# Work moved from VectorE to ScalarE and GpSimd, gate tiles last, retention states in two groups, in a hybrid decoder layer on one core

## Chip, cores and metric

One core of one Trainium2 chip runs the whole program in one launch. The metric is device microseconds of one execution. The kernel before takes 1557.36 us (median of 3 runs, 1556.4 to 1557.76).

## What is computed

One layer over 304 tokens: 16 meta tokens and 256 prompt tokens, and 8 samples of 4 new tokens. Columns of one input projection are split between two groups of heads (RWKV-7, 16 heads of 64; retention, 4 heads of 256), whose outputs go through one output projection; then a SwiGLU network. All in float32. The inner part, cut:

```python
z = rms_norm(x, norm_mix) @ w_in                      # 2048 -> 3360 + 4096 columns
o_a, S_a = rwkv7_mixer(z[..., :RWKV_COLS], z_prev, S_a0, ...)
o_b, S_b = retention_mixer(z[..., RWKV_COLS:], S_b0, pos, prompt)
h = x + concatenate([o_a, o_b]) @ w_out
h = h + (silu(hn @ w_gate) * (hn @ w_up)) @ w_down    # hn = rms_norm(h, norm_ffn), 2048 -> 5632 -> 2048
# RWKV-7, per step:  S = S * w_t + (S @ a_t) b_t + v_t k_t ;  out = S @ r_t
# retention, per chunk:
o = (q @ k.T * dmask) @ v + (q @ S) * inter_scale
S_new = exp(log_gamma * C) * S + (k * k_scale).T @ v
o = o * rsqrt(mean(o * o) + eps) * silu(g)
```

The outputs are y for prompt and samples, the last projected rows and the new states of both groups.

## The kernel before, in words

Activations lie transposed (features on partitions, the 304 tokens along the free dimension). The weights of all projections stand in one long array `big` in the order of their use, and are streamed by SP's queue in loads of 1024 columns (512 KB, tiles `wr`, three buffers, `load` at line 608). Each float32 weight is split: ScalarE casts 512 columns to a high half `wh` (`cast`, line 617), VectorE subtracts it from the weight and leaves a low half `wl` (`rest`, line 629). TensorE then makes three matmuls for each block of 128x128 weights: high x high, high x low activations, low x high (`main`, line 634). A piece of 512 columns is four blocks, 12 matmuls. In `main` the cast runs four pieces ahead; the subtraction follows in the middle of a piece and is needed two and a half pieces later.

`sequence` (line 103) gives the order of the output tiles. First come 59 tiles of the input projection: 3 for the LoRA inputs, then by `ORDER` (line 54) 3 tiles for each of 8 RWKV pairs of heads (p0 to p7), 6 for each retention head (r0 to r3: q, k, v), 2 for each head's gate (g0 to g3). After them come the output projection in two halves (the second needs the retention heads) and the feed-forward network.

Beside this main stream run the heads, as generators that give way at every `yield`. A planner (`Plan`, line 307) drafts the program first: it books each instruction with a duration on its engine's clock (`book`, line 348, for instance 265 + 2 n ns for a GpSimd product of n columns), steps a generator when its data are due, and lets the main stream go on otherwise. The order that comes out is written as it is; each engine works through its own queue in order. So a row of one engine that comes late holds whatever is queued behind it on that engine.

The parts that the change touches:
- `rsqrt` (line 705): a reciprocal root by an integer guess and two corrections, all on VectorE. Twelve calls are 288 wide (8 in `pair_out`, line 1297, and 4 in `ret`), 8 are 312 wide and have a floor in place of the affine first step (`pair`, line 906), one is 304 wide at the start, the others are 3 wide.
- `lora_weights` (line 870): splits a pair's LoRA weights in halves, twice for each pair, and loads the pair's sample states `s0`.
- `pair`: builds the padded operand `arp` (a and r, [128, 5, 2, 2, 64]) and multiplies it by `bku` to scores.
- `inverse` (line 1095): for each pair the inverse of triangular 64x64 blocks. VectorE reduces, then spreads a row by 15 shuffles in three groups of five; GpSimd makes two products or sums for each of them (30 rows of 5 to 75 columns); VectorE then masks, transposes and spreads the result (a 128x512 product), and TensorE multiplies.
- `sample` (line 1219): the sample tokens of a pair; VectorE scales `s0` there.
- `ret` (line 1379): a retention head. It loads four tiles of sample states (`s0r`, 512 KB each, by `states`, line 1390), multiplies q with them (16 matmuls into one PSUM tile), and later updates and stores the four tiles (`out_rts`). Head 0 starts after pair 3, head 1 after pair 5, heads 2 and 3 after pair 6, head h also after head h-2.

Since a wrapper (`Timed`, line 291) issues every instruction, all have one line in the profile, L302. Tiles of the heads lie in one arena, so their names there are `arena_dt.float` (or `arena_dt.float32r`); `acc` and `mm` are PSUM tiles of the main stream and of the heads.

Of the kernel before, what the change touches and what calls it, by code (L numbers as in the profile page):

```python
# [15 lines left out]
P = 128  # L16
# [3 lines left out]
META = 16  # L20
# [22 lines left out]
WARM = 10  # L43
BRIDGE = 4
# [9 lines left out]
ORDER = "p0 p1 g0 p2 r0 p3 p4 g1 p5 r1 p6 g2 p7 g3 r2 r3"  # L54
# [252 lines left out]
class Plan:  # L307
# [40 lines left out]
    def book(self, eng, what, a, k):  # L348
# [20 lines left out]
        else:  # L369
            part = out.shape[0] < P  # L370
            each = sum(math.prod(x.shape[1:]) == 1 for x in ins) if n > 1 else 0
            if eng == "DVE":
                big = max(math.prod(x.shape[1:]) for x in aps)
                per = 0.56 if what == "tensor_scalar" and ins[0].name not in self.banks else 1.05
                dur, tail = {"stream_shuffle": (148, 90), "transpose": (95 + 1.02 * n, 80), "tensor_reduce": (40 + 1.8 * big, 85),
                             "tensor_tensor_scan": (65 + 2.1 * n, 85)}.get(what, (62 + per * n + 67 * each, 83))
            elif eng == "ACT":
                dur, tail = 108 + 0.83 * n + 90 * each - 40 * (ins[0].name in self.banks), 94
            else:
                dur, tail = (60 + 0.85 * n, 60) if what == "memset" else (185 + 0.8 * n, 60) if what == "tensor_copy" else (265 + 2 * n, 60)  # L380
# [158 lines left out]
class Step:  # L539
# [165 lines left out]
    def rsqrt(self, src, scale, eps, floor=None, out=None):  # L705


        dve = self.dve
# [24 lines left out]
    def start(self):  # L733
# [3 lines left out]
        self.dve.memset(self.ones, 1.0)  # L737
        xh, xl = self.xh, self.xl
# [131 lines left out]
    def lora_weights(self, p, half, z):  # L870
# [4 lines left out]
        if not half:  # L875
            z["s0"] = self.t([P, NB, 64], "s0")
            self.sp.dma_start(z["s0"], self.I["s0w"][p])
# [5 lines left out]
        dve.tensor_sub(lo, lw, hi)  # L883
# [22 lines left out]
    def pair(self, p, z):  # L906
# [4 lines left out]
        while not all(("lora", i) in self.done for i in range(3)) or len(z) < 5:  # L911
            yield
# [6 lines left out]
        k, r, v, s0, (wh, wl) = z["k"], z["r"], z["v"], z["s0"], z["lora", 0]  # L919
# [46 lines left out]
        arp = self.t([P, NU, 2, 2, 64], "arp")  # L966
# [6 lines left out]
        pool.memset(arp[:, 0], 0.0)  # L973
        for hi, h in enumerate(HALF):
            pool.memset(arp[h, 1:, :, 1 - hi], 0.0)
# [15 lines left out]
        for hi, h in enumerate(HALF):  # L991
            act.copy(arp[h, 0, 0, hi, :META], ra[h, 0, :META])
            act.copy(arp[h, 1:, :, hi], units(ra[h]))
# [17 lines left out]
        for g in (1, 2), (3, 4), (0,):  # L1011
            pt = self.ps()
            n = 2 if g[0] else 1
            for j, u in enumerate(g):
                pe.matmul(pt[:, j * 2 * P:(j * 2 + n) * P], bku[:, u],
                          arp[:, u, :n].rearrange("p q h c -> p (q h c)"), start=True, stop=True)
# [21 lines left out]
        for i, h in enumerate(HALF):  # L1038
            act.copy(sc[h, :, 0, i, :], arp[h, :, 0, i, :])
# [7 lines left out]
        yield from self.units(p, sc, bkt, sv, sav, tt, arp, dl, o)  # L1047
# [47 lines left out]
    def inverse(self, mt):  # L1095
# [7 lines left out]
        pool.tensor_copy(x, cst("i16", 16)[:, None, :].to_broadcast([P, NU, 16]))  # L1103
        yield
# [4 lines left out]
        ems = []  # L1109
# [9 lines left out]
        for li in range(2):  # L1119
            em = self.t([P, NU, 64], "em")  # L1120
            pool.memset(em[:, NU - 1], 0.0)
            dve.tensor_mul(em[:, :NU - 1], mt[:, 1:],
                           cst("lvl", 128)[:, li * 64:(li + 1) * 64][:, None, :].to_broadcast([P, NU - 1, 64]))
            ems.append(em)
        yield
# [46 lines left out]
    def units(self, p, sc, bkt, sv, sav, tt, arp, dl, o):  # L1172
# [36 lines left out]
        for u in range(1, NU):  # L1209
            out = pt[:, (u - 1) * P:u * P]  # L1210
            pe.matmul(out, flat(sv, u), arp[:, u, 1].rearrange("p h c -> p (h c)"), start=True, stop=False)
# [7 lines left out]
    def sample(self, p, v, ax, axd, bs, d4, s0):  # L1219
# [10 lines left out]
        for hi, h in enumerate(HALF):  # L1230
            for b in range(2):
                act.copy(xs[h, b::2], pb[HALF[b], :, b, hi, :])

# [46 lines left out]
        dve.tensor_mul(s0, s0, d4.to_broadcast([P, NB, 64]))  # L1280
# [98 lines left out]
    def ret(self, h, q, k, v):  # L1379
# [50 lines left out]
        states()  # L1430
# [16 lines left out]
        pt = self.ps()  # L1447
        for g in range(2):
            for d in range(2):
                for j in range(4):  # L1450
                    b = 4 * g + j
                    pe.matmul(pt[32 * j:32 * j + 32, :RD], qz[:, d, b, :], s0s[b // 2][:, d, b % 2, :],
                              start=g + d == 0, stop=g + d == 2, tile_position=(0, 32 * j))

# [6 lines left out]
        qo = self.t([P, RD], "qo")  # L1461
        act.copy(qo, pt[:, :RD])
# [5 lines left out]
        act.copy(svh[0:32], svh[32:64].bitcast(F32))  # L1468

# [10 lines left out]


        for b2 in range(NB // 2):
            s0 = s0s[b2]
            vx = self.t([P, 2, RD], "vxr", F32R)
            for j in range(2):
                c = cst("bm128", 8)[:, 2 * b2 + j:2 * b2 + j + 1]
                if j:
# [282 lines left out]
```

## Time and profile before

| what | value |
|---|---|
| runs, median (3) | 1557.36 us |
| the profiled execution | 1558.99 us |
| its span, first to last instruction | 1557.1 us |
| TensorE's mean granted clock | 0.996 |
| weight loads | 409 of 512 KB and 8 of 256 KB |

The input projection with the heads takes about the first 587 us, the output projection follows, and from about 704 us on the feed-forward network. In a line of the waits stand: the engine and what it was to write, whom it waited for, then the sum in us, the number of waits and the longest. In a line of groups: line, engine, operation, out<-in, shape, count, busy us, mean ns of one, and idle time of the engine before them with what ended it. In a line of the timeline: start, length, engine, operation, count, and in brackets the idle time before it. In a line of stretches: the stretch and its length, then the busy time and count of PE, its weight loads (PEld), DVE (VectorE), ACT (ScalarE) and POOL (GpSimd), then the granted clock, the DMA share and GB/s.

### The profile page before, as it was taken

What the parts mean: (1) busy time and instruction counts of PE and PEld (TensorE: products, weight loads), DVE (VectorE), ACT (ScalarE), POOL (GpSimd) and SP (SyncE); (2) the same over time, 40 slices, a digit from 0 to 9 for tenths busy, and PEclk for the clock granted to TensorE, in tenths of its full rate; (3) what the DMA queues carried; (4) which work ended last, traced back from release to release, by engine and by line L of the source; (5) the groups of instructions that cost most, each with busy time, mean ns of one, the idle gap of its engine ahead of it and who ended that gap; (6) DMA issues with size and microseconds to landing.
All of it is one profiled execution on the core that took longest, in us unless ns stands there. A gap on an engine that the chain in (4) does not pass through costs nothing.

```text
span 1557.1 us, 30803 instructions
## 1 busy us (share of the span) xinstructions
PE 1535.6 (99%) x11388; PEld 1505.7 (97%) x11388; DVE 1102.0 (71%) x2590; ACT 821.4 (53%) x1795; POOL 179.2 (12%) x567
## 2 busy tenths in 40 slices
PE   9999999999999999999999999999999999999997
PEld 8999999998999999999999999999999999999997
DVE  7999888996999786676555565555565656565657
ACT  6766776766676555455444444444444444444445
POOL 0454415513143000000000000000000000000000
PEclk9999999999999999999999999999999999999999
DMA  7443443434545546755555555555555555555553
GB/s 249 154 136 119 127 130 120 115 107 152 181 143 176 170 143 238 243 167 161 164 173 163 174 156 172 162 165 169 168 163 172 164 166 164 171 166 166 161 176 118
DMA packets 76997, 252.48 MB, mean 162 GB/s; under 512 B 9392, under 2 KB 14640, under 8 KB 76848
## 3 DMA queue, kind: packets, MB, share of 16 engines
q1 hardware_dynamic: 76848, 250.52, 51.5%
q8 instruction: 90, 1.47, 0.4%
q14 instruction: 59, 0.48, 0.1%
HBM read 236.21 MB, written 14.28 MB: 161 GB/s over the span
## 4 chain that ended last, share of the span: by engine, by line
PE 85%; DVE 11%; issue 1%; ACT 1%; DMA 1%; POOL 0%; SPq 0%; DVEq 0%; ACTq 0%; POOLq 0%
PE acc L302 76%; PE mm L302 9%; DVE arena_dt.float L302 8%; DVE wl L302 3%; ACT arena_dt.float L302 1%; DMA arena_dt.float<-xT 0%; POOL arena_dt.float L302 0%; DMA arena_dt.float<-lora 0%; ACT wh L302 0%; DVE arena_dt.float32r L302 0%; DMA wr<-big 0%; ACT arena_dt.float32r L302 0%; SPq L302 0%; DVEq L1766 0%; ACT xh L302 0%
## 5 line engine op out<-in xcount | busy, mean ns | idle before, releaser
L302 PE MATMUL acc<-xh,wh 128*128 128x288 f32 (+2 forms) x2592 | 790.9, 305 | 0.0
L302 PE MATMUL acc<-xh,wl 128*128 128x288 f32 (+2 forms) x2592 | 769.9, 297 | 0.9 <-DVE wl L302 0.8
L302 PE MATMUL acc<-xl,wh 128*128 128x288 f32 (+2 forms) x2592 | 766.7, 296 | 0.0
L302 ACT CAST wh<-wr 128x512 fp32r<-128x512 f32 x826 | 501.6, 618 | 373.2 <-PE acc L302 343.3
L302 DVE TENSOR_TENSOR wl<-wr,wh 128x512 fp32r<-128x512 f32 x826 | 563.3, 690 | 114.5 <-ACT wh L302 112.1
L302 PEld LDWEIGHTS acc<-xh,wh 128*128 128x128 f32 x2592 | 487.7, 188 | 4.8 <-issue 1.5
L302 PEld LDWEIGHTS acc<-xl,wh 128*128 128x128 f32 x2592 | 486.9, 188 | 4.0 <-issue 0.7
L302 PEld LDWEIGHTS acc<-xh,wl 128*128 128x128 f32 x2592 | 486.0, 188 | 2.0 <-DVE wl L302 1.5
L302 PE MATMUL acc<-arena_dt.float32r,wh 128*128 128x288 f32 x1408 | 280.0, 294 | 0.4 <-ACT arena_dt.float32r L302 0.3
L302 PEld LDWEIGHTS acc<-arena_dt.float32r,wh 128*128 128x128 f32 x1408 | 225.5, 188 | 0.9 <-ACT arena_dt.float32r L302 0.6
L302 PE MATMUL acc<-arena_dt.float32r,wl 128*128 128x288 f32 x704 | 207.0, 294 | 0.0
L302 DVE TENSOR_TENSOR arena_dt.float<-acc,arena_dt.float 128x288 f32<-128x288 f32 (+4 forms) x181 | 72.7, 420 | 167.6 <-PE acc L302 167.3
L302 PE MATMUL mm<-arena_dt.float 128*128 128x128 f32 (+7 forms) x1072 | 168.4, 317 | 6.2 <-DVE arena_dt.float L302 4.9
L302 DVE TENSOR_TENSOR arena_dt.float<-arena_dt.float 128x288 f32<-128x288 f32 (+11 forms) x483 | 159.5, 354 | 11.7 <-ACT arena_dt.float L302 6.2
L302 DVE TENSOR_TENSOR arena_dt.float<-arena_dt.float,acc 128x288 f32<-128x288 f32 x208 | 94.4, 454 | 100.8 <-PE acc L302 100.6
L302 PEld LDWEIGHTS mm<-arena_dt.float 128*128 128x128 f32 (+1 forms) x1072 | 138.2, 182 | 20.6 <-issue 9.3
L302 ACT ACTIVATE arena_dt.float<-arena_dt.float 128x288 f32<-128x288 f32 (+6 forms) x200 | 85.0, 432 | 119.5 <-DVE arena_dt.float L302 118.2
L302 PEld LDWEIGHTS acc<-arena_dt.float32r,wl 128*128 128x128 f32 x704 | 132.7, 189 | 0.0
L302 ACT COPY arena_dt.float<-mm 64x64 f32<-64x64 f32 (+8 forms) x330 | 91.1, 287 | 72.6 <-PE mm L302 62.4
L302 POOL TENSOR_TENSOR arena_dt.float<-arena_dt.float 128x75 f32<-128x75 f32 (+14 forms) x240 | 94.5, 394 | 100.4 <-DVE arena_dt.float L302 75.6
L302 ACT CAST arena_dt.float32r<-arena_dt.float 128x288 fp32r<-128x288 f32 (+4 forms) x73 | 30.5, 424 | 102.2 <-DVE arena_dt.float L302 89.6
L302 POOL COPY arena_dt.float<-arena_dt.float 128x32 f32<-128x32 f32 (+5 forms) x123 | 35.6, 321 | 125.9 <-DVE arena_dt.float L302 74.0
(64 smaller groups left out, 676.0 us busy)
## 6 DMA issues: line engine op xcount, KB each, us to landing
wr<-big SPq DMA_DIRECT2D x409, 512.0 KB, 3.5
arena_dt.float<-s0r SPq DMA_DIRECT2D x16, 512.0 KB, 6.4
out_rts<-arena_dt.float SPq DMA_DIRECT2D x16, 512.0 KB, 5.4
arena_dt.float<-xT SPq DMA_DIRECT2D x4, 576.0 KB, 6.5
out_y<-arena_dt.float SPq DMA_DIRECT2D x8, 288.0 KB, 2.2
arena_dt.float<-xT SPq DMA_DIRECT2D x7, 304.0 KB, 5.6
wr<-big SPq DMA_DIRECT2D x8, 256.0 KB, 5.3
arena_dt.float<-lora SPq DMA_DIRECT2D x16, 128.0 KB, 3.7
```

Of the source, the lines that this page charges most:

```text
L302: return self._plan.keep(f(*a, **k))
```

## The change

Seven edits, and the planner's order that follows from them:
1. `rest`: a weight's low half is subtracted on GpSimd wherever the planner's clocks say that GpSimd is free and VectorE is behind (by more than `SLOW`); else on VectorE as before. In the order 86 of 826 go to GpSimd, 75 of them in the 59 tiles of the input projection.
2. `rsqrt`: calls wider than 64 take their affine step and the squares of the guess from ScalarE; the correction is written as y(c d - c x y y), two fused operations on VectorE each.
3. `lora_weights`, `inverse`, `sample`: the LoRA low halves, the two level masks and the scaling of `s0` go to GpSimd, and the two latter come earlier.
4. `inverse`: two sums replace the reduction, and a shuffle writes only the columns that are used.
5. `pair`: the padded operand lies in two tiles, `au` and `ru`; a score product of 256 columns becomes two of 128. The load of `s0` moves from `lora_weights` to the pair's start.
6. `ret`: q times the states goes in two groups of two state tiles, each group followed by its updates and stores; the second two tiles are loaded after the first group's products. The groups' products meet in a sum on VectorE.
7. `ORDER`: all gate tiles come after the last heads' tiles. Three constants of the planner's booking change as well.

```diff
+SLOW = 600
-ORDER = "p0 p1 g0 p2 r0 p3 p4 g1 p5 r1 p6 g2 p7 g3 r2 r3"
+ORDER = "p0 p1 p2 r0 p3 p4 r1 p5 r2 p6 p7 r3 g0 g1 g2 g3"
...
-                dur, tail = {"stream_shuffle": (148, 90), ...
+                dur, tail = {"stream_shuffle": (62 + 1.05 * n, 90), ...
...
-                ... (265 + 2 * n, 60)
+                ... (250 + 1.8 * n, 60)
...
     def rest(self):
         for r in self.rests:
-            self.dve.tensor_sub(*r)
+            c = self.plan.clock
+            idle = lambda: int(max(c["POOL"], c["PE"]) + SLOW < max(c["DVE"], c["PE"]))
+            (self.pool if self.plan.decide(idle) else self.dve).tensor_sub(*r)
...
     def rsqrt(self, src, scale, eps, floor=None, out=None):
...
+        wide = n > 64
         if floor is not None:
             dve.tensor_scalar(x, src, floor, None, op0=ALU.max)
+        elif wide:
+            act.activation(x, src, AF.Identity, scale=scale, bias=self.eps[eps][:m])
+            yield
         else:
             dve.tensor_scalar(x, src, scale, eps, op0=ALU.mult, op1=ALU.add)
...
-        dve.tensor_mul(a, x, y)
-        yield
-        dve.scalar_tensor_tensor(a, a, -0.703952253, y, op0=ALU.mult, op1=ALU.mult)
-        dve.scalar_tensor_tensor(y, a, 0.703952253 * 2.38924456, y, op0=ALU.add, op1=ALU.mult)
-        yield
-        dve.scalar_tensor_tensor(a, x, -0.5, y, op0=ALU.mult, op1=ALU.mult)
-        dve.tensor_mul(a, a, y)
-        yield
-        dve.scalar_tensor_tensor(y, a, 1.5, y, op0=ALU.add, op1=ALU.mult)
+        for c, d in (0.703952253, 2.38924456), (0.5, 3.0):
+            if wide:
+                yield
+                act.activation(a, y, AF.Square)
+                yield
+                dve.scalar_tensor_tensor(a, a, -c, x, op0=ALU.mult, op1=ALU.mult)
+            else:
+                dve.tensor_mul(a, x, y)
+                yield
+                dve.scalar_tensor_tensor(a, a, -c, y, op0=ALU.mult, op1=ALU.mult)
+            dve.scalar_tensor_tensor(y, a, c * d, y, op0=ALU.add, op1=ALU.mult)
...
     def lora_weights(self, p, half, z):
-        dve.tensor_sub(lo, lw, hi)
+        self.pool.tensor_sub(lo, lw, hi)
...
     def inverse(self, mt):
-        dve.tensor_reduce(rr, rb.rearrange("p u q c -> p u c q"), axis=AX.X, op=ALU.add)
+        dve.tensor_add(rb[:, :, :2], rb[:, :, :2], rb[:, :, 2:])
+        dve.tensor_add(rr, rb[:, :, 0], rb[:, :, 1])
...
-                dve.stream_shuffle(rs[:, s - c[0]], rr, [16 * (i // 16) + s for i in range(32)])
+                dve.stream_shuffle(rs[:, s - c[0], :, s + 1:], rr[:, :, s + 1:],
+                                   [16 * (i // 16) + s for i in range(32)])
...
     def ret(self, h, q, k, v):
-        states()
...
+        for g in range(2):
+            pt = self.ps()
...
+            if not g:
+                states()
+            yield
+            if g:
+                dve.tensor_add(qo, qo, pt[:, :RD])
+            else:
+                act.copy(qo, pt[:, :RD])
+            for b2 in range(2 * g, 2 * g + 2):
...
+                self.put(self.O["rts"][h, b2], s0)
```

Three places in the order. First GpSimd's queue in the middle of pair 0's inverse, before the change (`128x5x11` is a product of 5 units by 11 columns):

```order
L302 TENSOR_TENSOR arena_dt.float_70<-arena_dt.float_70 128x5x12 x2
L302 TENSOR_TENSOR arena_dt.float_70<-arena_dt.float_70 128x5x11 x2
L302 TENSOR_TENSOR arena_dt.float_70<-arena_dt.float_70 128x5x10 x2
L302 TENSOR_TENSOR arena_dt.float_70<-arena_dt.float_70 128x5x9 x2
L302 TENSOR_TENSOR arena_dt.float_70<-arena_dt.float_70 128x5x8 x2
```

The same place on GpSimd after the change (`wl` is a weight's low half, the `float32r` row the low half of LoRA weights):

```order
L303 TENSOR_TENSOR arena_dt.float_70<-arena_dt.float_70 128x5x12 x2
L303 TENSOR_TENSOR arena_dt.float_70<-arena_dt.float_70 128x5x11 x2
L303 MEMSET arena_dt.float_70 128x1
L303 COPY arena_dt.float_70<-arena_dt.float_70 128x8
L303 TENSOR_TENSOR wl_1137<-wr_1056,wh_1136 128x512
L303 TENSOR_TENSOR arena_dt.float_70<-arena_dt.float_70 128x5x10 x2
L303 TENSOR_TENSOR arena_dt.float_70<-arena_dt.float_70 128x5x9 x2
L303 TENSOR_TENSOR arena_dt.float_70<-arena_dt.float_70 128x5x8 x2
L303 TENSOR_TENSOR arena_dt.float_70<-arena_dt.float_70 128x5x7 x2
L303 TENSOR_TENSOR arena_dt.float_70<-arena_dt.float_70 128x5x6 x2
L303 TENSOR_TENSOR arena_dt.float32r<-arena_dt.float_70,arena_dt.float32r 128x256
L303 COPY shout_464<-arena_dt.float_70 128x1
```

A weight's low half and a LoRA low half now stand among the inverse's rows; low halves of weights stand behind the end of several other inverses too.

Second, VectorE's queue before the spread (`128x512`, which TensorE needs) of pair 5's inverse, before the change (`cst` are masks; `128x448` is the retention's mask of head 0, the `128x256` row its q for the samples):

```order
L302 TENSOR_TENSOR arena_dt.float_70<-arena_dt.float_70 128x8x2
L302 TENSOR_TENSOR arena_dt.float_70<-mm_5008,arena_dt.float_70 128x448
L302 TENSOR_TENSOR arena_dt.float_70<-arena_dt.float_70,cst_260 128x256 x2
L302 TENSOR_TENSOR arena_dt.float_70<-arena_dt.float_70,cst_260 128x160
L302 TENSOR_TENSOR arena_dt.float_70<-arena_dt.float_70,cst_260 128x320
L302 STREAM_TRANSPOSE arena_dt.float_70<-arena_dt.float_70 128x160
L302 TENSOR_TENSOR arena_dt.float_70<-arena_dt.float_70,cst_260 128x512
```

And after the change (`mm_5008` and `mm_5009` are state updates of head 0 now, `acc` a tile of the projection):

```order
L303 TENSOR_TENSOR arena_dt.float_70<-arena_dt.float_70,cst_266 128x160
L303 TENSOR_TENSOR arena_dt.float_70<-arena_dt.float_70,cst_266 128x320
L303 TENSOR_TENSOR arena_dt.float_70<-arena_dt.float_70 128x32
L303 TENSOR_SCALAR arena_dt.float_70<-arena_dt.float_70 128x288
L303 SCALAR_TENSOR_TENSOR arena_dt.float_70<-arena_dt.float_70,mm_5008 128x512
L303 SCALAR_TENSOR_TENSOR arena_dt.float_70<-arena_dt.float_70,mm_5009 128x512
L303 TENSOR_SCALAR arena_dt.float32r<-arena_dt.float32r,cst_266 128x256
L303 TENSOR_TENSOR wl_5039<-wr_4918,wh_5038 128x512
L303 STREAM_TRANSPOSE arena_dt.float_70<-arena_dt.float_70 128x160
L303 TENSOR_TENSOR arena_dt.float_70<-arena_dt.float_70 128x8x2x2
L303 TENSOR_TENSOR arena_dt.float_70<-acc_4917,arena_dt.float_70 128x304 x2
```

Head 0 has moved: its mask is done by then, and its state updates stand between the inverse's products where the retention's mask stood.

Third, SP's queue at the sample states of the third retention head, before the change (`wr` are weights):

```order
L302 DMA arena_dt.float_70<-rmask 128x448
L302 DMA out_rwp<-arena_dt.float_70 128x64
L302 DMA wr_7271<-big 128x1024
L302 DMA arena_dt.float_70<-s0r 128x1024 x4
L302 DMA wr_7388<-big 128x1024
L302 DMA out_rws<-arena_dt.float_70 128x512
L302 DMA wr_7467<-big 128x1024
```

The same place on SP after the change, where heads 2 and 3 start together:

```order
L303 DMA arena_dt.float_70<-rmask 128x448 x2
L303 DMA out_rwp<-arena_dt.float_70 128x64
L303 DMA wr_7347<-big 128x1024
L303 DMA wr_7403<-big 128x1024
L303 DMA arena_dt.float_70<-s0r 128x1024 x6
L303 DMA out_rws<-arena_dt.float_70 128x512
L303 DMA wr_7537<-big 128x1024
L303 DMA arena_dt.float_70<-s0r 128x1024 x2
L303 DMA wr_7613<-big 128x1024
```

Where four state tiles stood between two weight loads, six stand now, and all eight of the two heads have one weight load among them.

More of the change, by code (lines that the diff above doesn't have):

```diff
@@ L379, in book @@
             else:
-                dur, tail = (60 + 0.85 * n, 60) if what == "memset" else (185 + 0.8 * n, 60) if what == "tensor_copy" else (265 + 2 * n, 60)
+                dur, tail = (60 + 0.85 * n, 60) if what == "memset" else (185 + 0.8 * n, 60) if what == "tensor_copy" else (250 + 1.8 * n, 60)
             if part and eng != "POOL":
@@ L737, in start @@
         self.dve.memset(self.ones, 1.0)
+        self.eps = {}
+        for e in {RMS_EPS, GN_EPS, 4 * RMS_EPS}:
+            self.eps[e] = self.t([P, 1], f"eps{len(self.eps)}", pool=self.cp)
+            self.pool.memset(self.eps[e], e)
         xh, xl = self.xh, self.xl
@@ L910, in pair @@
             yield
-        while not all(("lora", i) in self.done for i in range(3)) or len(z) < 5:
+        while not all(("lora", i) in self.done for i in range(3)) or len(z) < 4:
             yield
@@ L1014, in pair @@
             for j, u in enumerate(g):
-                pe.matmul(pt[:, j * 2 * P:(j * 2 + n) * P], bku[:, u],
-                          arp[:, u, :n].rearrange("p q h c -> p (q h c)"), start=True, stop=True)
+                for q in range(n):
+                    c = (j * 2 + q) * P
+                    pe.matmul(pt[:, c:c + P], bku[:, u], flat(ru, u - 1) if q else flat(au, u), start=True, stop=True)
             yield
@@ L1445, in ret @@
         self.put(self.O["rtp"][h], so)
[L1447 to L1453, printed above, removed]
         skh = self.t([P, RD], "skh", F32R)
```

92 lines of the change are left out of this document (48 added, 44 removed).

## The prediction

> **What bounds the kernel now.** I read the page first, then each engine's busy time by stretch, then who keeps TensorE (PE) waiting.
>
> ```profile
> span 1557.1 us, 30803 instructions
> PE 1535.6 (99%) x11388; PEld 1505.7 (97%) x11388; DVE 1102.0 (71%) x2590; ACT 821.4 (53%) x1795; POOL 179.2 (12%) x567
> PE 85%; DVE 11%; issue 1%; ACT 1%; DMA 1%; POOL 0%; SPq 0%; DVEq 0%; ACTq 0%; POOLq 0%
> ```
>
> PE is busy 99% and holds 85% of the chain that ended last. The change leaves every weight matmul in place, so it can only win back time in which PE stands still. Where that is, the stretches say (columns: PE, PEld, DVE, ACT, POOL busy; clock; DMA):
>
> ```profile
> 40.00:565.00 525.00, 516.74 (x3739) 491.91 (x3737) 461.95 (x1401) 358.25 (x956) 178.09 (x556) 1.00 0.44 139
> 565.00:1547.00 982.00, 980.72 (x7411) 977.91 (x7409) 605.90 (x1128) 437.52 (x793) 0.00 (x0) 1.00 0.55 170
> 1200.00:1240.00 40.00, 40.00 (x305) 40.00 (x304) 24.52 (x45) 17.51 (x31) 0.00 (x0) 1.00 0.53 161
> ```
>
> From 565 us on PE loses 1.3 us in 982: nothing to win there. In the first stretch, input projection and heads, it loses 8.3 us, and VectorE (DVE) is busy 88%. PE's waits inside that stretch, with their sum, count and longest:
>
> ```profile
> PE mm L302 <- DVE arena_dt.float L302: 4.9, 5, 2.4
> PE mm L302 <- ACT arena_dt.float L302: 1.6, 2, 0.9
> PE acc L302 <- DVE wl L302: 0.8, 1, 0.8
> PE mm L302 <- POOL arena_dt.float L302: 0.3, 1, 0.3
> ```
>
> Nine waits, 7.6 us. A little more hides: 305 matmuls in 40 us start every 0.131 us, while each row lasts 0.30, so a wait begins some 0.17 us before it is booked (nine times: 1.5 us). The longest wait, on PE and on DVE at the same time, and the clock around it:
>
> ```profile
> 364.97 0.29 PE L302 MATMUL acc<-xh,wl 128*128 128x290 f32 x1
> 367.67 0.35 PE L302 MATMUL mm<-arena_dt.float 128*128 128x128 f32 x1 [2.41 <-DVE arena_dt.float L302]
> 362.51 1.94 DVE L302 TENSOR_TENSOR arena_dt.float<-arena_dt.float 128x16 f32<-128x16 f32 x9
> 365.14 1.40 DVE L302 TENSOR_TENSOR arena_dt.float<-arena_dt.float,cst 128x256 f32<-128x256 f32 x4
> 366.83 0.69 DVE L302 TENSOR_TENSOR arena_dt.float<-arena_dt.float,cst 128x512 f32<-128x512 f32 x1
> 365.50:368.50 3.00, 0.83 (x7) 0.86 (x8) 2.97 (x10) 0.87 (x2) 0.13 (x1) 1.00 0.99 386
> 369.00:372.00 3.00, 3.00 (x32) 1.31 (x24) 1.40 (x3) 1.37 (x4) 0.00 (x0) 0.50 0.93 250
> 360.00:400.00 40.00, 37.59 (x269) 33.11 (x267) 30.48 (x84) 27.14 (x79) 5.96 (x27) 0.96 0.37 111
> ```
>
> DVE is not idle there: it works off small products and the retention's masks ahead of the 128x512 product that PE needs, so the wait is a queue on DVE. Afterwards PE's clock is 0.50; over the 40 us the granted clock is 0.96, that is 1.6 us lost. Everything recoverable: 7.6 + 1.5 + 1.6 = 10.7 us. The page "TensorE: Matmul & The Clock Gate" of the Trainium skill (§ Why this matters for your kernels) allows idle gaps up to about 3 us without a loss of clock. The trace halves the clock after 2.41 us (and the 0.17 that hides), so the row decides, and the 1.6 stay in the sum; by the page only the wait itself would come back, and the forecast would be about 1 us less of a gain.
>
> **The change, part by part.** What leaves DVE, by the rows of the first stretch:
>
> ```profile
> L302 DVE TENSOR_TENSOR wl<-wr,wh 128x512 fp32r<-128x512 f32 x205 | 142.2, 695 | 19.4 <-ACT wh L302 19.1
> L302 DVE TENSOR_TENSOR arena_dt.float<-arena_dt.float 128x312 f32<-128x312 f32 x72 | 33.0, 478 | 0.5
> L302 DVE TENSOR_TENSOR arena_dt.float<-arena_dt.float 128x288 f32<-128x288 f32 x44 | 20.0, 465 | 0.8 <-ACT arena_dt.float L302 0.2
> L302 DVE TENSOR_SCALAR arena_dt.float<-mm 128x288 f32<-128x288 f32 x10 | 4.5, 453 | 2.0 <-PE mm L302 2.0
> L302 DVE TENSOR_TENSOR arena_dt.float<-arena_dt.float,cst 128x256 f32<-128x256 f32 x22 | 8.6, 433 | 1.1 <-POOL arena_dt.float L302 1.0
> L302 DVE TENSOR_TENSOR arena_dt.float32r<-arena_dt.float,arena_dt.float32r 128x256 fp32r<-128x256 f32 x16 | 6.7, 419 | 0.4 <-ACT arena_dt.float32r L302 0.4
> L302 DVE TENSOR_TENSOR arena_dt.float<-arena_dt.float 128x512 f32<-128x512 f32 x8 | 5.5, 682 | 0.1
> L302 DVE STREAM_SHUFFLE arena_dt.float<-arena_dt.float 128x80 f32<-128x80 f32 x120 | 20.8, 241 | 0.0
> L302 ACT ACTIVATE arena_dt.float<-arena_dt.float 128x288 f32<-128x288 f32 x16 | 7.1, 444 | 13.3 <-DVE arena_dt.float L302 13.2
> ```
>
> - Low halves of weights: 86 subtractions go to POOL, 75 in the input projection and about 66 in this stretch of it: 66 x 0.695 = 45.9 us.
> - Low halves of the 16 LoRA blocks, 16 level masks, 8 state scalings: 16 x 0.419 + 16 x 0.433 + 8 x 0.682 = 19.1 us.
> - Reciprocal roots: each of 12 wide ones loses an affine step and two products on DVE, 12 x (0.453 + 2 x 0.465) = 16.6; the 8 with a floor lose two products, 8 x 0.956 = 7.6. ACT gets 24 squares of 0.444, 16 of about 0.46 and 12 affine steps: some 23 us, so ACT goes from 358 to about 381 of 525 (73%).
> - Shuffles write 5 to 75 columns where they wrote 80. A shuffle's fixed part isn't shown alone: saving 0 to half of 20.8 us; I take 2.5. The reduce becomes two sums: about 1 us saved.
> - The split retention product adds four 256-wide sums, 1.7 us by the 0.433 row.
>
> Net: 45.9 + 19.1 + 24.2 + 3.5 - 1.7 = 91 us. DVE falls from 462 to 371, less what POOL beside it costs: single subtractions lasted up to 839 ns against a median of 686.
>
> ```profile
> L302 DVE TENSOR_TENSOR wl<-wr,wh x826: 640/686/839, 5.5 to 1538.5; 128x512 fp32r<-128x512 f32 x166
> L302 POOL MEMSET arena_dt.float<- 128x512 f32 x8 | 4.2, 525 | 0.0
> L302 POOL TENSOR_TENSOR arena_dt.float<-arena_dt.float 128x65 f32<-128x65 f32 x16 | 7.5, 469 | 1.3
> L302 POOL TENSOR_TENSOR arena_dt.float<-arena_dt.float 128x10 f32<-128x10 f32 x16 | 5.1, 317 | 1.3
> 348.74 5.01 POOL L302 TENSOR_TENSOR arena_dt.float<-arena_dt.float 128x75 f32<-128x75 f32 x10 [15.25 <-DVE arena_dt.float L302]
> 353.88 3.91 POOL L302 TENSOR_TENSOR arena_dt.float<-arena_dt.float 128x50 f32<-128x50 f32 x10
> 358.00 4.51 POOL L302 TENSOR_TENSOR arena_dt.float<-arena_dt.float 128x25 f32<-128x25 f32 x10
> ```
>
> That is a stretch of up to 22% while POOL works, 0 to 27 us on the 121 us that POOL gains (below); I take 10 (most subtractions lay near the median although POOL worked beside some of them), and DVE stands at 381, 73%.
>
> "GPSIMD Engine Reference" of the skill (§ 8, Key points) speaks against the change here: GpSimd shares its SBUF interfaces with VectorE and contends with VectorE instructions that read two SBUF inputs, which these subtractions do on both engines. The 839 agrees that it happens, the median of 686 that it is seldom; by the page all 27 us would be paid, DVE would stand at 398 (76%), and of the gain below 0.7 us would be lost.
>
> No row shows a 128x512 subtraction on POOL. A memset of that size, 0.525 us, bounds it below. From 10 to 65 columns a product grows from 317 to 469 ns, 2.76 ns a column; carried on to 512 that is 1.70 us. I take 1.3, nearer the upper end since it too reads two inputs. POOL's total becomes 178 + 66 x 1.3 + about 35 for the 40 smaller moves = 299 of 525, some 121 more: room enough on average, the question is its order.
>
> What this buys. Waits on DVE hold 4.9 + 0.8 us, six times 0.17 hidden, and the clock's 1.6: 8.3 us. How much of a queue stays when its server goes from 88% to 73%? As an estimate the queue goes with busy over idle: 7.3 before, 2.7 after, so a good third stays. Bounds: nothing gained (0) to all of it (8.3). I take two thirds, **-5.5 us**. What is late next is ACT and POOL.
>
> What it costs. The wide roots now hop DVE, ACT, DVE twice each; PE's two waits on ACT (1.6 us) may be none more or double: 0 to +1.6, **+0.4** taken. Queued behind a root's square on ACT are the casts of the weights' high halves, which run ahead of PE.
>
> The padded operand becomes two tiles, and 32 score products of 256 columns become 64 of 128:
>
> ```profile
> L302 PE MATMUL mm<-arena_dt.float 128*128 128x128 f32 x512 | 83.1, 279 | 5.0 <-DVE arena_dt.float L302 4.5
> L302 PE MATMUL mm<-arena_dt.float 128*128 128x256 f32 x144 | 36.3, 379 | 0.0
> ```
>
> Each counts as two rows: 64 x 0.252 = 16.1 against 128 x 0.162 = 20.8 us, at most +4.7; but the columns are the same and a row's tail overlaps the next matmul, so the floor is 0, and I take **+0.3**. A low half on POOL that comes late costs PE directly, see the rivals: 0 to +11, **+1.0** taken. Gates last, the retention two tiles at a time and the later load of the state change order only: 0, as long as PE has weight matmuls for cover (price below).
>
> Sum: -5.5 + 0.4 + 0.3 + 1.0 = -3.8 us on the span of 1557.1: 1553.3. The profiled execution took 1558.99, 1.89 around its span, and lies 1.63 above the median of 1557.36; so 1557.36 - 3.8 = **1553.6 us**.
>
> **The rivals.**
> - *All of it goes, nothing is added*: the DVE waits vanish and POOL's subtractions are always early: 1557.4 - 8.3 = 1549.1. For: POOL is 66% idle in this stretch; against: it runs in order.
> - *Slower: low halves late on POOL.* The order puts them between and behind the inverse's products. The planner books 250 + 1.8 n ns for one: 30 of them with 1200 columns are 9.7 us. The trace took 5.01 + 3.91 + 4.51 = 13.4. So POOL comes 3.8 us late to a subtraction behind an inverse. The main loop orders it 2.5 pieces of 12 matmuls ahead, 30 x 0.131 = 3.9 us, less its own 1.3: 2.6 us of slack. From a lateness of 2.6 us on PE waits: 3.8 - 2.6 = 1.2, with the hidden 0.17 1.4 us; at eight inverses 11 us in place of the +1.0: 1557.4 - 5.5 + 0.7 + 11 = 1563.6. For: these rows, and that it repeats. Against: a late POOL cost PE only 0.3 us before, and VectorE's products, which stretch POOL's, grow fewer.
> - *Weights late behind the states.* Both last heads now load together: six blocks of 512 KB and one of 256 between two weight loads, where four stood.
>
> ```profile
> wr<-big SPq DMA_DIRECT2D x409, 512.0 KB, 3.5
> arena_dt.float<-s0r SPq DMA_DIRECT2D x16, 512.0 KB, 6.4
> ```
>
>   3.4 MB at the 386 GB/s of a full stretch (0.99, above) is 8.8 us, and 3.5 for the next load: 12.3. Three loads ahead cover 3 x 24 x 0.131 = 9.4. Short by 2.9, with the clock 4.5 us: 1558.1. Against: the two heads' own matmuls lengthen the cover just there.
> - *It doesn't do what it says*: the planner packs the streams anew, other queues stand in front of PE, and the waits only change place: 1557.4.
>
> **How the numbers follow.** Forecast 0.42 (its own range 1550 to 1557), all goes 0.18, late low halves 0.22, late weights 0.10, no effect 0.08. About 0.2%, 3.1 us, is what a measurement of this kernel can tell from no change: faster means under 1554.2, slower over 1560.5. Faster: 0.31 of the forecast's 0.42 and all 0.18, 0.49. Same: 0.11 + 0.02 of the late low halves + 0.06 of the late weights + 0.08, 0.27. Slower: 0.20 + 0.04, 0.24. The range runs from 1547.5 (below "all goes", towards the 10.7 us that are there at most) to 1562.5; it leaves out the lowest end and the upper half of the late low halves, not 0.2 in all.
>
> **What would show it.** Right: DVE about 381 us in the first stretch, PE's waits on DVE there under 2.5 us, a clock of 1.00 around 367 us, POOL about 299 us with subtractions of 1.0 to 1.7 us, and PE's waits on POOL's low halves under 1.5. Wrong: a row "PE acc <- POOL wl" of several us (late low halves); ACT's casts waiting for the weights' DMA while the last heads load (late weights); DVE down by 80 us and PE's waits unchanged (no queue after all).

## The result: 51 us slower

The kernel after takes 1607.88 us (median of 4 runs, 1607.4 to 1608.98), the kernel before, on the same chip, 1556.88 (4 runs). The ratio is 1.033, 95% interval 1.0312 to 1.0347. The profiled execution of the kernel after took 1607.4 us, with a span 48.5 us longer than before. Its page:

```profile
span 1605.6 us, 31068 instructions
PE 1549.7 (97%) x11452; PEld 1515.0 (94%) x11452; DVE 1085.4 (68%) x2421; ACT 845.1 (53%) x1866; POOL 315.4 (20%) x712
```

The stretches, by the prediction's borders:

```profile
40.00:565.00 525.00, 485.50 (x3464) 461.56 (x3464) 421.85 (x1194) 344.33 (x928) 276.00 (x668) 0.98 0.41 126
565.00:1547.00 982.00, 980.34 (x7391) 972.99 (x7390) 596.41 (x1100) 446.32 (x834) 28.11 (x24) 1.00 0.56 172
365.50:368.50 3.00, 3.00 (x21) 2.83 (x20) 3.00 (x9) 1.94 (x7) 2.12 (x11) 1.00 0.62 240
```

From 565 us on nothing is lost, and the old wait at 367 us is gone, as forecast. But in the first stretch PE now stands still for 39.5 us (8.3 before), although DVE is busy for 40 us less (in part because PE runs late and the stretch holds less of the work). PE's waits there:

```profile
PE mm L303 <- DVE arena_dt.float L303: 25.6, 19, 2.7
PE mm L303 <- ACT arena_dt.float L303: 4.5, 6, 1.3
PE mm L303 <- DVE arena_dt.float32r L303: 3.8, 2, 2.1
PE acc L303 <- POOL wl L303: 2.4, 1, 2.4
PE mm L303 <- POOL arena_dt.float L303: 1.8, 1, 1.8
PE acc L303 <- DVE wl L303: 1.1, 1, 1.1
```

Thirty waits, 39.2 us; with 0.17 hidden at each, 5.1 more. The clock drops to half for 3.4 us in five places; the first and the last of the five 40-us stretches that show it:

```profile
40.00:80.00 40.00, 37.52 (x260) 36.82 (x259) 33.71 (x69) 27.34 (x63) 23.65 (x53) 0.96 0.50 152
520.00:560.00 40.00, 36.88 (x259) 35.64 (x260) 28.71 (x98) 22.71 (x66) 22.06 (x65) 0.96 0.41 125
```

That is 5 x 1.6 = 8 us. By the prediction's own count, 39.2 + 5.1 + 8 = 52.3 us are lost where 10.7 were: 41.6 of the 48.5; the rest is too small a piece at a time for a row.

Why does PE wait for an engine with more room? The groups of DVE in the first stretch tell. Three shapes of the kernel before (the second number behind the bar is the mean duration in ns):

```profile
L302 DVE SCALAR_TENSOR_TENSOR arena_dt.float<-arena_dt.float 128x288 f32<-128x288 f32 x44 | 20.3, 465 | 0.3
L302 DVE TENSOR_TENSOR arena_dt.float<-arena_dt.float,cst 128x320 f32<-128x320 f32 x16 | 7.8, 488 | 8.0 <-ACT arena_dt.float L302 8.0
L302 DVE TENSOR_TENSOR arena_dt.float<-arena_dt.float,cst 128x512 f32<-128x512 f32 x16 | 11.0, 690 | 0.3
```

The same three after, and two groups with an input in PSUM (`mm`, `acc`):

```profile
L303 DVE SCALAR_TENSOR_TENSOR arena_dt.float<-arena_dt.float 128x288 f32<-128x288 f32 x33 | 22.3, 676 | 2.3 <-ACT arena_dt.float L303 1.7
L303 DVE TENSOR_TENSOR arena_dt.float<-arena_dt.float,cst 128x320 f32<-128x320 f32 x16 | 15.5, 970 | 13.5 <-ACT arena_dt.float L303 11.3 <-issue 2.2
L303 DVE TENSOR_TENSOR arena_dt.float<-arena_dt.float,cst 128x512 f32<-128x512 f32 x16 | 15.1, 946 | 0.3
L303 DVE TENSOR_TENSOR arena_dt.float<-mm,cst 128x512 f32<-128x512 f32 x16 | 11.0, 687 | 1.0 <-PE mm L303 0.6 <-issue 0.3
L303 DVE TENSOR_TENSOR arena_dt.float<-acc,arena_dt.float 128x304 f32<-128x304 f32 x24 | 10.5, 464 | 2.0 <-PE acc L303 1.9
```

The same work takes up to twice as long, but only with both inputs in SBUF; with one in PSUM nothing has changed (683 and 468 before). One place shows how, at 350 us, on POOL, DVE and PE (start, length, and in brackets the idle time before):

```profile
350.27 2.75 POOL L303 TENSOR_TENSOR wl<-wr,wh 128x512 fp32r<-128x512 f32 x2 [7.19 <-ACT wh L303]
354.69 1.52 POOL L303 TENSOR_TENSOR wl<-wr,wh 128x512 fp32r<-128x512 f32 x1 [1.67 <-ACT wh L303]
```

```profile
350.32 3.02 DVE L303 SCALAR_TENSOR_TENSOR arena_dt.float<-arena_dt.float 128x288 f32<-128x288 f32 x2
353.26 0.81 DVE L303 TENSOR_TENSOR arena_dt.float<-acc,arena_dt.float 128x288 f32<-128x288 f32 x2
354.61 1.92 DVE L303 SCALAR_TENSOR_TENSOR arena_dt.float<-arena_dt.float 128x288 f32<-128x288 f32 x2
357.27 0.57 DVE L303 SCALAR_TENSOR_TENSOR arena_dt.float<-mm,arena_dt.float 64x64 f32<-64x64 f32 x2
```

```profile
357.99 0.46 PE L303 MATMUL mm<-arena_dt.float 128*128 128x128 f32 x2 [1.23 <-DVE arena_dt.float L303]
```

Two products that take 0.9 us alone last 3.02 beside two subtractions on POOL (1.28 and 1.52 us), and two others 1.92, of which the second began beside one. Each of these three ended 0.32 us after the subtraction: it stands until POOL's instruction has ended. A pair's 64x64 recurrence queues behind them on DVE, and PE waits 1.23 us for it. How long POOL's instruction is, its row over the whole trace shows (least, median and most, ns):

```profile
L303 POOL TENSOR_TENSOR wl<-wr,wh x86: 1260/1328/2253, 5.7 to 1566.2; 128x512 fp32r<-128x512 f32 x86
```

Counted over the whole trace, 70 DVE instructions, 63 with two SBUF inputs and 7 tensor_scalars from SBUF to SBUF, started while such a subtraction ran (20 ns after its start to 150 ns before its end); 64 of them (58 and 6) lasted over 0.1 us longer than usual. Of 50 others (an input in PSUM, shuffles, transposes) none did.

From here on "lengthened" is the sum, between 20 and 645 us, of what DVE's instructions with their inputs in SBUF last above the lower fifth of their own shape's durations, where that is over 60 ns. It is 6.6 us before and 80.5 after, 57.7 of it beside low halves of weights.

### The profile page after: what moved, and what is told of

Its sections match the earlier page's. It is cut to its first block, busy times and chain, and to the rows that moved or that the text cites. A ratio compares the mean times of both kernels' runs of the same rounds, so it can differ in the third digit from the quotient of the medians.

```text
span 1605.6 us, 31068 instructions
## 1 busy us (share of the span) xinstructions
PE 1549.7 (97%) x11452; PEld 1515.0 (94%) x11452; DVE 1085.4 (68%) x2421; ACT 845.1 (53%) x1866; POOL 315.4 (20%) x712
## 4 chain that ended last, share of the span: by engine, by line
PE 64%; DVE 4%; ACT 1%; issue 1%; DMA 0%; DVEq 0%; POOL 0%; POOLq 0%; ACTq 0%; SPq 0%
PE acc L303 61%; DVE arena_dt.float L303 3%; PE mm L303 3%; DVE wl L303 0%; ACT arena_dt.float L303 0%; DMA wr<-big 0%; ACT arena_dt.float32r L303 0%; ACT xh L303 0%; ACT wh L303 0%; DVE arena_dt.float32r L303 0%; DVE xl L303 0%; DVEq L1789 0%; POOL arena_dt.float L303 0%; POOLq L303 0%; ACTq L303 0%
## 5 line engine op out<-in xcount | busy, mean ns | idle before, releaser
L303 DVE TENSOR_TENSOR wl<-wr,wh 128x512 fp32r<-128x512 f32 x740 | 506.9, 694 | 133.6 <-ACT wh L303 126.3
L303 POOL TENSOR_TENSOR wl<-wr,wh 128x512 fp32r<-128x512 f32 x86 | 122.7, 1432 | 1080.2 <-ACT wh L303 1021.8
L303 ACT ACTIVATE arena_dt.float<-arena_dt.float 128x288 f32<-128x288 f32 (+6 forms) x242 | 103.4, 435 | 144.7 <-DVE arena_dt.float L303 141.9
L303 DVE TENSOR_TENSOR arena_dt.float<-arena_dt.float 128x288 f32<-128x288 f32 (+13 forms) x449 | 173.6, 414 | 8.3 <-ACT arena_dt.float L303 4.3
L303 PEld LDWEIGHTS mm<-arena_dt.float 128*128 128x128 f32 (+1 forms) x1136 | 142.5, 183 | 36.3 <-issue 12.3
L303 ACT COPY arena_dt.float<-mm 64x64 f32<-64x64 f32 (+11 forms) x330 | 91.5, 286 | 74.5 <-PE mm L303 68.9
L303 POOL TENSOR_TENSOR arena_dt.float<-arena_dt.float 128x70 f32<-128x70 f32 (+15 forms) x248 | 90.4, 365 | 25.0 <-DVE arena_dt.float L303 7.6
```

The costliest lines, as they stand in the source:

```text
L303: return self._plan.keep(f(*a, **k))
```

## The experiments

Theory L, the lock, says that this holding makes the chains of the heads late, against an order made without it. Rivals are O (the order of the tiles), P (POOL itself delivers late), and, for the lock's price, S against I: surprise, or longer chains in any order. The kernel before took 1558 us beside all of these.

| run | lengthened, us | time, us | ratio to before |
|---|---|---|---|
| e1 low halves on VectorE | 22.2 | 1573.5 | 1.0099 (1.0083 to 1.0115) |
| e2 memsets on GpSimd | 24.4 | 1560.3 | 1.0014 (1.0004 to 1.0023) |
| e3 copies on GpSimd | 58.0 | 1586.8 | 1.0187 (1.0170 to 1.0204) |
| e4 old order | 83.8 | 1613.1 | 1.0355 (1.0339 to 1.0371) |
| e5 nothing moved to GpSimd | 5.5 | 1554.5 | 0.9976 (0.9967 to 0.9985) |
| e6 after, lock booked | 101.2 | 1597.0 | 1.0246 (1.0230 to 1.0261) |
| e7 before + edit 1 | 73.7 | 1612.3 | 1.0347 (1.0333 to 1.0361) |
| e8 e5, lock booked | 5.5 | 1551.2 | 0.9956 (0.9942 to 0.9969) |
| e9 e1, lock booked | 24.2 | 1563.7 | 1.0035 (1.0022 to 1.0049) |
| e10 before, lock booked | 3.9 | 1579.7 | 1.0143 (1.0130 to 1.0157) |
| e11 e5, roots on VectorE | 6.3 | 1558.1 | 1.0002 (0.9993 to 1.0011) |
| e12 e8, old order | 6.1 | 1554.9 | 0.9984 (0.9975 to 0.9993) |

**e1.** In `rest`:

```diff
-            (self.pool if self.plan.decide(idle) else self.dve).tensor_sub(*r)
+            self.dve.tensor_sub(*r)
```

> The kernel after with all low halves of weights back on VectorE (edit 1 undone alone). Theory L (lock): a VectorE instruction with two inputs in SBUF that comes up while GpSimd runs an instruction that reads SBUF stands until that one ends; after's trace has 80.5 us of such lengthening between 20 and 645 us, 57.7 of it beside low halves of weights and 16.3 beside the other long moved instructions. By L the loss of 51 us shrinks with it: 51 x 16.3 / 74 = 11 us stay, about 1568 us (1558 to 1578), and lengthened VectorE time falls to about 23 us. Theory O (order: gates last and the heads closer together leave TensorE without cover): the order of the tiles is the same, so it stays at 1595 or more. Theory P (GpSimd itself hands low halves over late): with none left on GpSimd, the loss is gone altogether, 1550 to 1557.

34 of the 51 us are gone, with the lengthened time at 22.2 us as L has it, the time 5 us above L's value and inside its range. O and P fall: the order of the tiles was the same, and the loss was not gone altogether.

**e2.** The same place, with the booking and so the order unchanged:

```diff
+            self.plan.book("POOL", "tensor_sub", r, {})
+            for w in (512, 512, 128):
+                self.plan.keep(self.nc.gpsimd.memset(lo[:, :w].bitcast(F32), 0.0))
```

> The kernel after, every instruction of TensorE, VectorE, ScalarE and SyncE in the same order, but each low half that GpSimd made is now three memsets there (512, 512 and 128 columns, by the rows 0.525 + 0.525 + 0.206 = 1.26 us against 1.27 for an undisturbed subtraction): GpSimd writes as long, but reads nothing. The low parts of these 86 pieces of weights are left out (zeros). L: nothing holds VectorE's two-input instructions beside them any more, 57.7 us of lengthening go, about 1565 us (1557 to 1575); products with two SBUF inputs beside a memset keep their usual time (0.45 to 0.69 us), one-input instructions may still be longer. P and O: GpSimd is as busy and the order is the same, 1600 to 1612.

Its stretch and POOL's memsets, then three of its groups on DVE:

```profile
40.00:565.00 525.00, 515.45 (x3797) 493.61 (x3796) 398.16 (x1251) 376.92 (x1015) 267.40 (x809) 1.00 0.45 143
```

```profile
L640 POOL MEMSET wl<- 128x512 f32 x134 | 71.2, 532 | 65.6 <-PE acc L303 54.8 <-issue 6.8
```

```profile
L303 DVE SCALAR_TENSOR_TENSOR arena_dt.float<-arena_dt.float 128x288 f32<-128x288 f32 x40 | 18.3, 459 | 3.2 <-ACT arena_dt.float L303 2.5
L303 DVE TENSOR_TENSOR arena_dt.float<-arena_dt.float,cst 128x512 f32<-128x512 f32 x16 | 11.0, 687 | 0.3
L303 DVE TENSOR_TENSOR arena_dt.float<-arena_dt.float,cst 128x320 f32<-128x320 f32 x16 | 9.0, 561 | 13.6 <-ACT arena_dt.float L303 11.4 <-issue 2.2
```

This decides it. The order of every queue is that of the kernel after (on POOL with three memsets for each subtraction), POOL is about as busy (267 against 276 us), and still 48 of the 51 us are gone: where POOL reads nothing, DVE's products are back at 459 and 687 ns. (The 561 of the third row come from two of the 16, of 1.07 us each, beside level masks on POOL.) The memsets also wait for no cast and come earlier; but PE's waits for POOL's low halves were 2.4 us in the kernel after, too little to matter here. And they don't read `wr`: SP's queue waited 67.8 us for POOL's subtractions in the first stretch after the change, 1.8 here; but no cast waited for a weight load in that stretch of the kernel after, and e3, which doesn't read `wr` either, is slow again.

The sum of lengthened time is not the price by itself: e1 and e2 have about the same, 22.2 and 24.4 us, and lie 13 us apart. DVE is 26 us busier in e1's first stretch and the order is another; which of the two makes the 13 us is open.

**e3.** Two copies, `gpsimd.tensor_copy(lo, hi)`, in place of the memsets.

> The kernel after in the same order, but each low half that GpSimd made is two copies of the high half (512 columns each, one input), so the low parts of these 86 pieces are left out. It asks what it takes to hold VectorE: if one SBUF input on GpSimd is enough, VectorE's two-input instructions are again lengthened to the end of the copy, and the loss goes with the copies' own length: as an estimate from 185 ns + 0.8 ns a column, the sum that the planner books for a copy, two copies are 1.19 us, close to the 1.27 of the subtraction, but a held instruction waits for one copy (0.6 us) and not for the whole: 1575 to 1600. If it takes two inputs on both sides: as with memsets, 1557 to 1575.

```profile
L640 POOL CAST wl<-wh 128x512 fp32r<-128x512 f32 x128 | 93.2, 732 | 93.1 <-ACT wh L303 73.2 <-issue 10.4 <-PE acc L303 5.4
L303 DVE SCALAR_TENSOR_TENSOR arena_dt.float<-arena_dt.float 128x288 f32<-128x288 f32 x38 | 21.6, 570 | 2.5 <-ACT arena_dt.float L303 1.9
```

One input read by POOL is enough to hold DVE, and two short holds cost less than one long one: 1586.8, between memsets and subtractions.

**e4.** `ORDER` as before.

> The kernel after with the old order of the tiles (edit 7 undone alone). L: the instructions on GpSimd and VectorE are the same, some 60 to 75 low halves still go to GpSimd in the input projection, so the loss stays: 1595 to 1615, with about 70 to 85 us of lengthened VectorE time. O: with the gate tiles back between the heads the waits go, 1555 to 1570.

1613 us: the order is not the cause; if anything the new one is better.

**e5.** `self.dve` in `rest`, `dve.tensor_sub` in `lora_weights`, level masks and state scaling on `dve` at their old places.

> The kernel after with everything that went to GpSimd back on VectorE in its old place: the low halves of the weights, those of LoRA, the level masks and the scaling of the sample states (edit 1 and all of edit 3 undone). Left are the roots over ScalarE, the shorter shuffles, the split operand, the retention in two groups and the gates last. L (lock): no long GpSimd instruction is left, the lengthened VectorE time falls to about the 6.6 us of before, and with some 28 us less work on VectorE than before the time is 1552 to 1559. O and the hops over ScalarE: the first experiment stood 15 us above the kernel before with its low halves already back; if the other edits made that, it stays at 1565 to 1575.

```profile
40.00:565.00 525.00, 521.23 (x3855) 499.53 (x3854) 441.32 (x1372) 380.92 (x1025) 170.11 (x570) 1.00 0.45 143
```

1554.5 us, faster than before. The other five edits are not the loss; together they gain 0.24%. From e1 this kernel differs by edit 3 alone, with the order that follows: 19 us.

**e6.** In `Plan.book` (cut; a GpSimd product is also booked with 265 + 2 n again):

```diff
+            wide = [x for x in ins if math.prod(x.shape[1:]) > 1 or n == 1]
+            lock = eng == "POOL" and ins or eng == "DVE" and not any(x.name in self.banks for x in aps) and (
+                what == "tensor_scalar" or len(wide) > 1 and what != "tensor_tensor_scan")
+            if lock:
+                for a, b in self.locks["DVE" if eng == "POOL" else "POOL"][-60:]:
+                    if a <= self.started < b:
+                        self.started = b + 30
+                self.locks[eng].append((self.started, self.started + dur))
```

> The kernel after, but the planner books the lock: a VectorE instruction with two inputs in SBUF, or a tensor_scalar from SBUF to SBUF, starts no earlier than a GpSimd instruction with an input ends, and the other way round; a GpSimd product is booked with 265 + 2 n ns again. The work is the same, only the order follows the true times; since VectorE's clock now runs behind more often, 117 in place of 86 low halves go to GpSimd. S (surprise: the lock costs because the order was made for times that don't hold, and VectorE with its room could wait): TensorE's waits on VectorE fall from 27 us to under 10, 1560 to 1580, although the lengthened time stays at 80 us or grows. I (intrinsic: products that wait for each other lengthen every head's chain, whatever the order): 1595 to 1620.

```profile
40.00:565.00 525.00, 504.81 (x3667) 483.34 (x3667) 432.12 (x1180) 352.02 (x938) 326.97 (x698) 0.99 0.41 129
565.00:645.00 80.00, 72.00 (x482) 61.42 (x481) 56.46 (x123) 52.39 (x137) 12.80 (x13) 0.96 0.62 212
```

1597: at the lower edge of I. PE's standing still in the first stretch is halved, 39.5 to 20.2 us, though the lengthened time grew to 101; but the heads end later, and 8 us of it come back after 565 us. It looks like part surprise, more longer chains; but more low halves moved too, and the parts can't be told apart.

**e7.** Edit 1 alone on the kernel before.

> The kernel before with edit 1 alone: 100 low halves of weights go to GpSimd where the planner's clocks let them. L: 57.7 us of lengthening stood beside 71 low halves of the first stretch; 71 x 100 / 86 = 83 of them make about 67 us, at 51 / 74 us of time for each that is +46: 1604 (1590 to 1615). If edit 1 needs the other edits to hurt (the retention's groups, the gates last): 1555 to 1575.

1612 us with 73.7 us lengthened, 68.0 of it beside low halves: edit 1 alone, with 100 of them against 86, loses as much as the whole change.

**e8.** e5 with e6's booking.

> The fifth kernel (nothing moved to GpSimd) with the planner that books the lock, which here concerns GpSimd's small products of the inverses alone (some 6 us of lengthening in the kernel before). S: TensorE's few waits in the first stretch fall a little, 1550 to 1557, and below the fifth kernel by 0 to 4 us. I: no difference to the fifth kernel beyond 2 us either way.

```profile
40.00:565.00 525.00, 524.46 (x3877) 506.81 (x3875) 440.34 (x1366) 380.59 (x1025) 177.19 (x570) 1.00 0.46 146
```

PE stands still for 0.5 us in 525. 1551.2 us is the best kernel here, 0.44% under the kernel before; the slowest of its 5 runs, 1551.6, is below the fastest of e5's 11, 1553.4, so the new booking gains some 3 us here.

**e9.** e1 with e6's booking.

> The first experiment (all low halves of weights on VectorE, the LoRA low halves, level masks and state scaling on GpSimd) with the planner that books the lock. The same instructions run on the same engines as there, only their order follows the booked lock. S: the 15 us that the first experiment stood above the kernel before were TensorE's waits for chains that came later than booked; with 16 us of lengthening booked they go, 1551 to 1560. I: the held products cost whatever the order, 1568 to 1576.

```profile
40.00:565.00 525.00, 520.08 (x3854) 504.44 (x3853) 436.75 (x1316) 375.50 (x1009) 214.72 (x609) 1.00 0.45 143
565.00:720.00 155.00, 150.45 (x1111) 142.32 (x1110) 112.92 (x238) 84.68 (x177) 0.22 (x1) 0.99 0.60 195
```

Between S and I: 10 us better than e1 with the same instructions on each engine and as much lengthened, 5.7 above before. In the first stretch PE stands still for 4.9 us, and 4.5 have moved to the end of the input projection.

**e10.** The kernel before with e6's booking.

> The kernel before, its planner booking the lock (it concerns GpSimd's small products of the inverses beside VectorE). Is the gain of the eighth kernel the booking's or the edits'? If the booking's: TensorE's nine waits of 7.6 us in the first stretch go from the kernel before too, 1550 to 1554. If it needs VectorE's relief (462 to 440 us): 1555 to 1559.

Neither: 22 us slower, with hardly anything lengthened. PE waits on ACT here, the longest time at 427 us; POOL, ACT and PE at that place:

```profile
424.53 1.51 POOL L302 MEMSET arena_dt.float<- 64x512 f32 x4 [6.15 <-DVE arena_dt.float L302]
```

```profile
426.35 0.43 ACT L302 COPY arena_dt.float<-mm 64x64 f32<-64x64 f32 x2 [3.17 <-POOL arena_dt.float L302]
```

```profile
426.92 0.46 PE L302 MATMUL mm<-arena_dt.float 128*128 128x128 f32 x2 [3.52 <-ACT arena_dt.float L302]
```

A memset of a pair's padded operand waits 6.15 us for DVE on POOL; ACT's copy of another pair's recurrence then waits for POOL, and PE for ACT. A memset has no input, so it waits for the arena's space. That the new order left the arena too little room is argued, not tried; the booking is no gain by itself. Since it can cost this much in another way, e6 does not tell how much of the loss stays with a known lock, and S against I remains open.

**e11.** e5 with the old `rsqrt`.

> The fifth kernel with the reciprocal roots on VectorE as before (edit 2 undone too). It asks whether what is taken off VectorE buys time at all, as the prediction had it: the roots over ScalarE take 24 us off VectorE. If the queue on VectorE is what TensorE waits for, the kernel goes back by most of the fifth's gain of 3.6 us, 1556 to 1559; if the gain came from the order (gates last, retention in groups, other booking), it stays at 1553 to 1556.

The two stretches of e11, and the second one of e5 (its first is above):

```profile
40.00:565.00 525.00, 521.31 (x3841) 501.98 (x3839) 453.97 (x1407) 363.11 (x977) 179.21 (x571) 1.00 0.46 145
565.00:720.00 155.00, 153.05 (x1157) 149.09 (x1157) 118.66 (x246) 80.13 (x162) 0.00 (x0) 1.00 0.60 193
```

```profile
565.00:720.00 155.00, 154.56 (x1155) 153.38 (x1155) 111.48 (x227) 81.95 (x163) 0.00 (x0) 1.00 0.62 200
```

Back to 1558.1: the roots over ScalarE take 19.8 us off DVE (454.0 + 118.7 against 441.3 + 111.5), and theirs is the gain of e5. It shows in the second stretch, where PE stands still for 1.95 us in place of 0.44, and in fewer matmul rows of the first.

**e12.** e8 with the old `ORDER`.

> The eighth kernel with the old order of the tiles (edit 7 undone). With the lock out of the way and TensorE standing still for only 1 us of the first stretch, the place of the gates should matter little: within 3 us of the eighth kernel's 1551.2. In the fourth experiment, with the lock, the old order was 5 us slower than the new; if the gates last serve as cover for the last heads, the same 5 us show here, 1555 to 1557.

1554.9: 3.7 us slower than e8, between both expectations. Gates last are worth some 4 us.

## Why the prediction was wrong

The failed step is the price of POOL's work beside DVE: "a stretch of up to 22% while POOL works, 0 to 27 us on the 121 us that POOL gains (below); I take 10". Its row, 839 against 686 ns, came from POOL's small products of 0.3 to 0.4 us, which could hold an instruction only that long: the 839 ns stand beside one of 371 ns. The ratio was carried over to instructions of 1.3 us, where it is not a ratio: a product waits out the whole subtraction. DVE came to 422 us and not to 381; by the prediction's sum the price was 422 - 371 = 51 us, beyond both ends. That is still too low, since PE ran late and the stretch held 191 weight subtractions (129 on DVE, 62 on POOL) where it had 205: counted by instruction, as "lengthened" above, it is 70.7 us in this stretch against 6.4 before. The second half of the failure is that it was paid as busy time only. DVE, busy 80% of the stretch, had room for it; but the order was made without it, and holds of about 1 us fell on chains that PE waits for.

- *DVE relief, -5.5 us.* It pays when nothing locks: the roots, 19.8 us of DVE against 24.2 forecast, gave 3.6 us (e5 against e11). In the change itself PE's waits on DVE grew from 5.7 to 30.5 us (25.6 + 3.8 + 1.1).
- *ACT's hops, +0.4.* e5 has them all and is faster, with 1.4 us of waits on ACT; that after's 4.5 us come from late chains is argued from this.
- *Score products, +0.3, and two groups of states, 0.* Not tried alone; both are in e5.
- *Low halves late on POOL, +1.0, and the rival of 1563.6.* POOL was judged about rightly: 276 us against 299, the subtraction 1.43 us on average within 1.0 to 1.7 (1.27 undisturbed, 1.3 taken); PE's one wait of 2.4 us is over the 1.5 named. The rival's side was right, its mechanism wasn't.
- *Late weights, the rival of 1558.1.* They did not come: the last two heads' states are loaded from 582 to 590 us, and no cast waits for a weight load between 5 and 639 us.
- *Order changes 0.* Gates last are a gain of some 4 us (e8 against e12); the new order is not what cost.

The prediction weighed a sentence on contention from "GPSIMD Engine Reference" of the Trainium skill, and used it for a share. The skill's page "SBUF — State Buffer" (§ Who interferes with whom) says more: the pair of ports is an exclusive lock for the whole instruction, and a VectorE instruction with two SBUF inputs contends with a GpSimd instruction that reads SBUF, not with one that only writes it. The runs agree: of the instructions with two SBUF inputs 58 of 63 were held beside subtractions, and beside e2's memsets none of 93.

## What to carry to other kernels

Before moving work to GpSimd, ask what VectorE runs at that time: here GpSimd's subtractions and copies, which read SBUF, held VectorE's products of two SBUF inputs until their own end, while products with a PSUM input and shuffles kept their time, and so did two-input products beside GpSimd's memsets. Price such a move also as lateness of the chain that waits, by the longest hold, and not only as a share of busy time. A row of small instructions bounds the price of long ones only if it is known whether the cost is a ratio or a wait.

## What the runs showed of the hardware

- A tensor_scalar from SBUF to SBUF is held even beside e2's memsets: 9 of 14 by over 0.1 us, 0.16 us on average.
- The hold goes both ways: POOL's longest subtraction, 2.25 us at 48.06 us where 1.27 is usual, ran beside two products with two SBUF inputs on DVE (at 48.26 and 48.63 us) that kept their usual time.
- The clock fell to half after shorter waits than the 2.41 us of before, but not after each. Behind the first of these two waits the clock was 0.50 from 73.7 us on, behind the second it stayed at 1.00:

```profile
73.08 0.46 PE L303 MATMUL mm<-arena_dt.float 128*128 128x128 f32 x2 [1.80 <-POOL arena_dt.float L303]
```

```profile
398.86 0.47 PE L303 MATMUL mm<-arena_dt.float32r 128*128 128x512 f32 x1 [2.08 <-DVE arena_dt.float32r L303]
```

What tells them apart is a raster: half clock begins only at borders a multiple of 3.41 us apart (73.7, 101.0, 261.4, 302.4 and 520.8 us here) and lasts one such stretch. The 1.80 us lie within one stretch; of the 2.08 us, 1.18 lie in one and 0.90 in the next. In all traces of this case, leaving out the first and the last 20 us, every stretch in which PE stood still for 1.80 us or more was followed by half clock, and of those with less only one was (1.61 us, in e9).
